# Where a hybrid decoder step casts and splits its weights around a norm: last lower parts behind the last residual sum, the memory's parts behind the inverse root

## The chip, the cores and the metric

The kernel runs on one core of a Trainium2 chip. The time is the device time of one launch in microseconds (us); the kernel before was timed in three runs, and one more execution was recorded by the hardware profiler. TensorE (PE) multiplies, VectorE (DVE), ScalarE (ACT) and GpSimd (POOL) do the elementwise work, SyncE (SP) issues the loads.

## The reference

One step of a decoder trunk of two layers over a prompt of 256 rows and 8 single sample rows, which share the weights (so 264 columns go through each projection). All of it is float32.

```python
def rmsnorm(x, g):
    y = x * lax.rsqrt(jnp.mean(x * x, axis=-1, keepdims=True) + EPS)
    return y * g

def cross_attn(x, mk, mv, w_q, w_o):
    q = (x @ w_q).reshape(B, T, X_HEADS, X_HEAD_DIM)          # 4 heads of 256
    s = jnp.einsum('bthd,bnhd->bhtn', q, mk) / math.sqrt(X_HEAD_DIM)
    p = jax.nn.softmax(s, axis=-1)
    o = jnp.einsum('bhtn,bnhd->bthd', p, mv).reshape(B, T, D)
    return o @ w_o
...
# layer i, D = 1024, D_FF = 2816:
x += 0.5 * swiglu(rmsnorm(x, norm_ffn1[i]), ...)
x += short_conv_mixer(...) if i is even else hgrn2_mixer(...)   # of rmsnorm(x, norm_mix[i])
x += cross_attn(rmsnorm(x, norm_xattn[i]), mk, mv, ...)
x += 0.5 * swiglu(rmsnorm(x, norm_ffn2[i]), ...)
# the prompt's mk, mv = split(rmsnorm(mem_prompt, norm_mem[i]) @ w_kv[i]); the samples' come from a cache
```

## The kernel before

The activations stand transposed, as xT of 8 tiles of 128 features by 264 columns. PE multiplies in float32r, a rounded float32, and each float32 product is made of three: high times high, low times high and high times low (mm3, lines 330 to 332: `wh`·`xh`, `wh`·`xl`, `wl`·`xh`). So every operand is kept as a rounded part (named with h) and the remainder (with l).

The weights come in parts of 512 KB by SP (raw). ACT casts each to its rounded part (wh, line 107), and DVE, or in some stages GpSimd, subtracts to get the lower part (wl, line 120). The class Weights does this ahead of use: the program is written as one sequence of products, and after every few of them `flow.tick()` is called, which first lets the weights `advance()` by one split, one cast and some loads, and then takes one step of each of three lists of generators (lanes). The emission order and a scheduler that keeps data dependences set the order on each engine. `W.behind(engine, instruction)` adds an order on one engine, without a wait: the instruction stands behind the one noted in `W.after[engine]`.

A norm is spread over the work around it. When a residual tile xT[k] is summed (by `evac` in `out_proj`, line 825, or in `ffn`, line 817), `nxt.kt(k)` makes its high part (ACT, line 350), its low part (DVE, line 355) and its square (ACT, line 366; POOL adds the squares into nacc, line 367). After the last tile the generator `finish` is started on lane 2: three ticks later ACT rounds the sum (nhi, line 376) and DVE makes its remainder (nlo, line 377), one tick later PE sums over the features (ps_ms, lines 380 and 381), ACT takes the logarithm and the exponential for the inverse root (line 310), where the next stage needs another function set loads it (a table load, line 306: silu for the ffn norms, sigmoid for the mixer norm of layer 1; the other three norms here load none), and DVE does a Newton step in three instructions (lines 321, 325, 326) that give R. The projections do not wait for R: their columns are scaled by R when a bank of PSUM is evacuated (g in `ffn`, qT at line 927). `project` starts the first two chunks of 256 output features interleaved, which takes all four banks named "mm"; the third chunk needs an evacuated bank. `out_proj` of attention goes through `project_late`, which multiplies the first three heads of the input before the last.

In `attention`, `mem_split` (lines 909 to 922) makes high and low parts of the memory on ACT (mh, line 918) and DVE (ml, line 919), `do_kv` makes keys and values of the prompt's memory from them for each head (kv, lines 941 to 943), and `sample_scores` reduces the cached keys on DVE (line 995, 128 reductions). `sample_rest` goes on with pst (lines 1069 to 1080), spv (line 1097, products with the cached values in groups of 32), copies to os (line 1108), transposes spt (line 1112), and oh and ol (lines 1115, 1116), which the output projection needs. pkt, psc, ppt and po belong to the prompt's heads.

Of the kernel before, what the change touches and what calls it, by code (L numbers as in the profile page):

```python
# [11 lines left out]
AF = mybir.ActivationFunctionType  # L12
ALU = mybir.AluOpType
# [5 lines left out]
KT = D // P  # L19
# [18 lines left out]
W_BUFS = 5  # L38
# [18 lines left out]
class Weights:  # L57


    def __init__(self, nc, pool):  # L60
        self.nc, self.pool = nc, pool
        self.halves, self.chunks = [], []
        self.raw, self.ready = {}, {}
        self.n_load = self.n_round = self.n_split = self.first_live = self.pos = 0
        self.lo, self.hi = ("v",), ("s",)
        self.pin = lambda ins: ins
        self.order, self.after = None, {}

    def add(self, *srcs):

# [63 lines left out]

    def advance(self):
        n = len(self.halves)
        if self.n_split < self.n_round:
            self._split()
        if self.n_round < n and self.n_round - self.first_live < W_BUFS:
            self._round()  # L140
        while self.n_load < n and self.n_load - self.n_split < RAW_BUFS:
            self._load()
# [97 lines left out]
def trunk_step(ctx: ExitStack, tc: tile.TileContext, ins, consts, outs, stop=None):  # L240
    nc = tc.nc
# [11 lines left out]
    def aux_bank(name):  # L253
        return paux.tile([P, 512], F32, tag="aux", name=name)

    W = Weights(nc, wp)
# [22 lines left out]
    memT = cp.tile([P, KT, NMEM], F32, name="memT")  # L279
    xh = cp.tile([P, KT, NC], F32R, name="xh")  # L280
    xl = cp.tile([P, KT, NC], F32R, name="xl")

    def gcol(name, layer, kt):
        r = ROW0[name] + layer
        return gains[:, kt, r : r + 1]
# [18 lines left out]
    def use_set(name):  # L304
        if loaded[0] != name:
            in_line(nc.scalar.preload_act_table_set(name))
            loaded[0] = name
# [4 lines left out]
    def rsqrt(dst, src, scale=1.0):  # L312

        n = dst.shape[0]
        use_set(LNEXP)
        act(dst, src, AF.Ln, bias=eps_t[:n], scale=scale)
        act(dst, dst, AF.Exp, scale=-0.5)

    def newton(dst, src, tmp, scale=1.0, out=None):
        if scale == 1.0:  # L320
            nc.vector.scalar_tensor_tensor(tmp, src, EPS, dst, op0=ALU.add, op1=ALU.mult)
        else:
            nc.vector.tensor_scalar(tmp, src, scale, EPS, op0=ALU.mult, op1=ALU.add)
            nc.vector.tensor_mul(tmp, tmp, dst)
        nc.vector.scalar_tensor_tensor(tmp, tmp, -0.5, dst, op0=ALU.mult, op1=ALU.mult)
        return nc.vector.scalar_tensor_tensor(dst if out is None else out, tmp, 1.5, dst, op0=ALU.add, op1=ALU.mult)
# [7 lines left out]
    class Norm:  # L334
# [17 lines left out]
        def low(self, k, src=None, n=NC):  # L352
            src = xT[:, k] if src is None else src
            g, h = gcol(self.name, self.layer, k), xh[:, k, :n].bitcast(F32)
            W.pin(nc.vector.scalar_tensor_tensor(xl[:, k, :n], src, g, h, op0=ALU.mult, op1=ALU.subtract))  # L355

        def split(self, k, src, n):
            self.high(k, src, n)
# [12 lines left out]
        def finish(self):  # L371
            yield
            yield
            yield
            hi, lo = (cp.tile([P, NC], F32R, tag="nsq", name=n, bufs=2) for n in ("nhi", "nlo"))
            nc.scalar.copy(hi, self.acc)
            nc.vector.tensor_sub(lo, self.acc, hi.bitcast(F32))
            yield
            ps = aux_bank("ps_ms")
            nc.tensor.matmul(ps[:, :NC], ones_d, hi, start=True, stop=False)  # L380
            nc.tensor.matmul(ps[:, :NC], ones_d, lo, start=False, stop=True)
            with tc.high_priority(offset=HURRY):
                rsqrt(self.R, ps[:, :NC])
                W.after["s"] = last[0]
                if self.after is not None:
                    use_set(self.after)
                W.after["v"] = newton(self.R, ps[:, :NC], self.acc).ins
            self.done = True
# [64 lines left out]
    def project_late(nch, rh, rl, evac, k0, ready):  # L453

        lead = 3
        first = W.chunks[W.pos]
        ws = [W.get_late() for _ in range(lead)]
        pss = [[(mm_bank if c < 2 else aux_bank)(f"pj{c}_{j}") for j in range(2)] for c in range(lead)]

        def block(c, k):  # L460
            for j in range(2):
                mm3(pss[c][j][:, :NC], ws[c](k), rh[:, k], rl[:, k], k == 0, k == KT - 1, slice(j * P, j * P + P))

        for k in range(k0):
            for c in range(2):
                block(c, k)
            if k == HK - 1:
                W.first_live = first[0] + 2
            flow.tick()
        for k in range(k0):  # L470
            block(2, k)
            if k == HK - 1:
                W.first_live = first[1]
            if k % 2:
                flow.tick()
        ready()

        def leave(c, j, ps):
            with tc.high_priority(offset=HURRY):
                evac(c, j, ps[:, :NC])  # L480

        def finish(c):
            for k in range(k0, KT):
                block(c, k)
            W.first_live = first[1] + c + 1
            for j in range(2):
                leave(c, j, pss[c][j])
            flow.tick()

        for c in range(lead - 1):  # L490
            finish(c)
        w = W.get_late()
        for j in range(2):
            ps = mm_bank(f"pj{lead}_{j}")
            for k in range(KT):
                mm3(ps[:, :NC], w(k), rh[:, k], rl[:, k], k == 0, k == KT - 1, slice(j * P, j * P + P))
                if k == KT // 2 - 1:
                    flow.tick()
            if j == 1:
                W.release()  # L500
            leave(lead, j, ps)
            flow.tick()
            if j == 0:
                finish(lead - 1)
# [315 lines left out]
            flow.drain(1)  # L820

    def out_proj(rh, rl, nxt, before=None, late=None):
        def evac(c, j, ps):
            k = 2 * c + j
            add = nc.vector.tensor_add(xT[:, k], xT[:, k], ps)
            if k == KT - 1:
                W.after["v"] = add.ins
                nxt.low(k - 1)
            nxt.kt(k, low=k != KT - 2)

        if late is not None:
            project_late(4, rh, rl, evac, *late)
        else:
            project(4, rh, rl, evac, before=before)


    def conv(norm, nxt):
        with tc.tile_pool(name="cv", bufs=1) as vp:
# [54 lines left out]

            flow.spawn(0, states())
            out_proj(yh, yl, nxt)
            flow.drain(0)


    def attention(l, norm, nxt):
        with tc.tile_pool(name="at", bufs=1) as ap:  # L900
            mh = ap.tile([P, KT, NMEM], F32R, name="mh")
# [11 lines left out]
            def mem_split():  # L913
                for _ in range(6):
                    yield
                for k in range(KT):
                    g = gcol("norm_mem", l, k)
                    nc.scalar.activation(mh[:, k], memT[:, k], AF.Copy, scale=g)
                    nc.vector.scalar_tensor_tensor(
                        ml[:, k], memT[:, k], g, mh[:, k].bitcast(F32), op0=ALU.mult, op1=ALU.subtract  # L920
                    )
                    yield

            def evac_q(h, j, ps):
# [137 lines left out]
            def sample_rest():  # L1062
# [53 lines left out]
                nc.vector.tensor_sub(olv, ptv, ohv.bitcast(F32))  # L1116

            flow.spawn(1, mem_split())
            project(XH, xh, xl, evac_q, need=norm)
            W.lo = ("p",)  # L1120
            for h in range(XH):
                do_kv(h)
            flow.drain(0)
            W.lo = ("v",)
            out_proj(oh, ol, nxt, late=(KT - 2, lambda: flow.drain(1)))


    GH = 4

    def rec(norm, nxt):  # L1130
        with tc.tile_pool(name="rc", bufs=1) as rp:
# [303 lines left out]
            def before(k):  # L1435
                while k not in made:
                    flow.step()

            out_proj(lambda k: yh[k // GH][:, k % GH], lambda k: yl[k // GH][:, k % GH], nxt, before=before)

    def states():
# [109 lines left out]
    for i, e in enumerate(plan):  # L1551
        if i + 1 < len(plan):
            nxt = Norm(*plan[i + 1][:3])
        else:
            nxt = Final() if stop is None else Stop()
# [60 lines left out]
```

## Time and profile before

| | before |
|---|---|
| time, median of 3 runs | 1294.13 us (1294.10 to 1295.05) |
| profiled execution: time | 1294.04 us |
| its span | 1292.3 us |
| granted TensorE clock | 0.998 |
| PE busy | 1270.8 us, 98% of the span |
| DVE, ACT, POOL busy | 824.0, 691.8, 293.3 us |
| bytes moved | 270.98 MB, mean 210 GB/s |

The span is the time from the first to the last instruction on the core. A row of the timeline has the start, the duration, the engine, the line and operation, the tile written and those read, and in brackets how long the engine was idle before it and what ended that. Rows of several like instructions carry their count (x3). In a list of waits the columns are the time in total, how often, and the longest. Matmul rows overlap (0.28 us long, started every 0.12).

### The profile page before, as it was taken

The page shows a single profiled execution, that of the slowest core. Times are in us where ns is not written, and L with a number is a line of the kernel's source. Part 1 is how long each engine was busy: PE and PEld are TensorE (multiplying, and loading weights), DVE is VectorE, ACT ScalarE, POOL GpSimd, SP SyncE. Part 2 cuts the span into 40 slices and gives each one's busy share as a digit, 9 for nine tenths or more (in the row PEclk, how much of TensorE's full clock was granted, in tenths as well). Part 3 has the DMA queues.
Part 4 walks back from the last instruction along what each step waited for, and adds up shares of the span by engine and source line. Part 5 has one row for each costly group of instructions (what it writes and reads, how often), then busy time and mean ns, then how long its engine had stood idle before and what let it go on. Part 6 is the DMA issues. An engine that isn't in the chain of part 4 may idle for free.

```text
span 1292.3 us, 25853 instructions
## 1 busy us (share of the span) xinstructions
PE 1270.8 (98%) x10267; PEld 1232.6 (95%) x10267; DVE 824.0 (64%) x1560; ACT 691.8 (54%) x1131; POOL 293.3 (23%) x237
## 2 busy tenths in 40 slices
PE   8999999999999999999999999999999999999996
PEld 8999999999869999999999999999998789999996
DVE  7555567759926755546655545887888628766454
ACT  6454545446545655544645544656575546766542
POOL 3211231212650211132111132000023531112220
PEclk9999999999999999999999999999999999999999
DMA  8796555646998666556666556563547995997551
GB/s 279 236 304 180 166 181 181 198 147 196 358 369 254 187 175 189 174 163 196 188 181 179 185 167 194 172 194 108 189 151 242 392 359 149 291 314 240 163 164 35
DMA packets 263755, 270.98 MB, mean 210 GB/s; under 512 B 8777, under 2 KB 259721, under 8 KB 261074
## 3 DMA queue, kind: packets, MB, share of 16 engines
q1 hardware_dynamic: 257726, 263.98, 64.4%
q10 hardware_dynamic: 5908, 5.35, 1.2%
q8 instruction: 81, 1.33, 0.4%
q14 instruction: 40, 0.33, 0.1%
HBM read 259.19 MB, written 10.10 MB: 208 GB/s over the span
## 4 chain that ended last, share of the span: by engine, by line
PE 92%; DVE 4%; ACT 2%; issue 1%; DMA 0%; POOL 0%; DVEq 0%; SPq 0%; ACTq 0%; POOLq 0%
PE pj L330 19%; PE pj L331 19%; PE pj L332 19%; PE dn L330 7%; PE dn L332 7%; PE dn L331 7%; PE kv L942 2%; PE kv L941 2%; PE kv L943 2%; DVE xl L355 2%; DVE wl L120 1%; PE spv L1097 1%; PE psc L1023 1%; PE pl L1263 1%; PE pj L408 1%
## 5 line engine op out<-in xcount | busy, mean ns | idle before, releaser
L120 DVE TENSOR_TENSOR wl<-raw,wh 128x1024 fp32r<-128x1024 f32 (+1 forms) x347 | 424.6, 1229 | 242.8 <-ACT wh L107 230.0
L330 PE MATMUL pj<-xh,wh 128*128 128x264 f32 x1952 | 558.4, 286 | 5.0 <-DVE qT L927 2.6
L331 PE MATMUL pj<-xl,wh 128*128 128x264 f32 x1952 | 553.3, 284 | 0.0
L332 PE MATMUL pj<-xh,wl 128*128 128x264 f32 x1952 | 553.1, 283 | 0.0
L107 ACT CAST wh<-raw 128x1024 fp32r<-128x1024 f32 (+1 forms) x406 | 415.9, 1032 | 251.2 <-PE pj L331 123.1
L330 PEld LDWEIGHTS pj<-xh,wh 128*128 128x128 f32 x1952 | 367.7, 188 | 7.3 <-DVE qT L927 3.0
L331 PEld LDWEIGHTS pj<-xl,wh 128*128 128x128 f32 x1952 | 367.9, 189 | 0.0
L332 PEld LDWEIGHTS pj<-xh,wl 128*128 128x128 f32 x1952 | 366.2, 188 | 0.0
L330 PE MATMUL dn<-ah,wh 128*128 128x264 f32 x704 | 200.9, 285 | 0.0
L332 PE MATMUL dn<-ah,wl 128*128 128x264 f32 x704 | 200.0, 284 | 0.0
L331 PE MATMUL dn<-al,wh 128*128 128x264 f32 x704 | 199.5, 283 | 0.0
L120 POOL TENSOR_TENSOR wl<-raw,wh 128x1024 fp32r<-128x1024 f32 (+1 forms) x61 | 142.9, 2351 | 183.9 <-ACT wh L107 120.0
L791 POOL TENSOR_TENSOR al<-a,ah 128x264 fp32r<-128x264 f32 x88 | 89.2, 1015 | 412.6 <-ACT ah L790 412.4
L332 PEld LDWEIGHTS dn<-ah,wl 128*128 128x128 f32 x704 | 132.7, 188 | 0.0
L330 PEld LDWEIGHTS dn<-ah,wh 128*128 128x128 f32 x704 | 132.4, 188 | 0.2
L331 PEld LDWEIGHTS dn<-al,wh 128*128 128x128 f32 x704 | 132.5, 188 | 0.0
L310 ACT ACTIVATE g<-g 128x264 f32<-128x264 f32 x88 | 37.0, 424 | 76.2 <-DVE g L783 76.0
L790 ACT CAST ah<-a 128x264 fp32r<-128x264 f32 x88 | 36.0, 413 | 70.4 <-DVE a L789 70.1
L350 ACT ACTIVATE xh<-xT,gains 128x264 fp32r<-128x264 f32 x56 | 28.2, 513 | 74.2 <-DVE xT L817 59.2
L995 DVE CUSTOM_DVE_ANT_0 junk<-ring,pq 128x256 f32<-128x256 f32 x128 | 53.6, 419 | 3.7
L783 DVE TENSOR_TENSOR g<-pj,R_norm_ffn 128x264 f32<-128x264 f32 x88 | 37.4, 429 | 28.7 <-PE pj L332 28.3
L789 DVE TENSOR_TENSOR a<-g,pj 128x264 f32<-128x264 f32 x88 | 37.0, 424 | 26.7 <-PE pj L332 26.7
(325 smaller groups left out, 1477.4 us busy)
## 6 DMA issues: line engine op xcount, KB each, us to landing
raw<-in_w_ffn_gate_dram SPq DMA_DIRECT2D x88, 512.0 KB, 6.0
raw<-in_w_ffn_up_dram SPq DMA_DIRECT2D x88, 512.0 KB, 3.9
raw<-in_w_ffn_down_dram SPq DMA_DIRECT2D x64, 512.0 KB, 3.5
ring<-in_cache_mem_k_dram SPq DMA_DIRECT2D x16, 1024.0 KB, 8.7
raw<-in_w_xkv_dram SPq DMA_DIRECT2D x64, 256.0 KB, 3.9
ring<-in_cache_mem_v_dram SPq DMA_DIRECT2D x16, 1024.0 KB, 8.5
raw<-in_w_rec_in_dram SPq DMA_DIRECT2D x32, 512.0 KB, 4.4
raw<-in_w_ffn_down_dram SPq DMA_DIRECT2D x32, 384.0 KB, 3.0
```

The source lines that it names most:

```text
L107: self.pin(self.behind(self.hi[i % len(self.hi)], copy(wh[:, :n], self.raw[i][:, :n])))
L120: ins = eng.tensor_sub(wl[:, :n], self.raw.pop(i)[:, :n], wh[:, :n].bitcast(F32))
L310: in_line(nc.scalar.activation(dst, src, func, **kw))
L330: nc.tensor.matmul(ps, wh[:, s], rh, start=first, stop=False)
L331: nc.tensor.matmul(ps, wh[:, s], rl, start=False, stop=False)
L332: nc.tensor.matmul(ps, wl[:, s], rh, start=False, stop=last)
L350: W.pin(nc.scalar.activation(xh[:, k, :n], src, AF.Copy, scale=gcol(self.name, self.layer, k)))
L783: nc.vector.tensor_mul(g, ps, norm.R)
L789: nc.vector.tensor_mul(a, g, ps)
L790: nc.scalar.copy(ah[:, blk], a)
L791: nc.gpsimd.tensor_sub(al[:, blk], a, ah[:, blk].bitcast(F32))
L995: nc.vector.tensor_tensor_reduce(junk, t[:, i % 8], pq[:, :XD], 1.0, 0.0, ALU.mult, ALU.add, sc[:, h, i : i + 1])
```

## The change

Three edits. `W.held` is set between the step of `finish` that makes nhi and nlo and the step with ps_ms, and no weight part is cast or split in between. In `out_proj`, the low parts of the last tiles (6 and 7; in attention's projection 4 to 7) stand behind the last residual sum. The memory's high parts stand behind the norm's exponential and its low parts behind the Newton step.

```diff
     def advance(self):
         n = len(self.halves)
-        if self.n_split < self.n_round:
+        if not self.held and self.n_split < self.n_round:
             self._split()
-        if self.n_round < n and self.n_round - self.first_live < W_BUFS:
+        if not self.held and self.n_round < n and self.n_round - self.first_live < W_BUFS:
             self._round()
...
             nc.vector.tensor_sub(lo, self.acc, hi.bitcast(F32))
+            W.held = True
             yield
+            W.held = False
             ps = aux_bank("ps_ms")
...
     def out_proj(rh, rl, nxt, before=None, late=None):
+        later = range(KT - 2 if late is None else KT - 4, KT - 1)
+
         def evac(c, j, ps):
             k = 2 * c + j
             add = nc.vector.tensor_add(xT[:, k], xT[:, k], ps)
+            nxt.kt(k, low=k < later[0])
             if k == KT - 1:
                 W.after["v"] = add.ins
-                nxt.low(k - 1)
-            nxt.kt(k, low=k != KT - 2)
+                for i in (*later, k):
+                    W.behind("v", nxt.low(i))
...
-                    nc.scalar.activation(mh[:, k], memT[:, k], AF.Copy, scale=g)
-                    nc.vector.scalar_tensor_tensor(
+                    W.behind("s", nc.scalar.activation(mh[:, k], memT[:, k], AF.Copy, scale=g))
+                    low = nc.vector.scalar_tensor_tensor(
                         ml[:, k], memT[:, k], g, mh[:, k].bitcast(F32), op0=ALU.mult, op1=ALU.subtract
                     )
+                    W.behind("v", low)
                     yield
```

What that moves in the order of the engines is shown at three places of layer 0. A name carries the number of its buffer, which differs between the two programs where it is a written one; a raw with the same number is the same weight part. Line numbers of after are one to seven higher (mh stands at line 924 there, spv at 1104, spt at 1119).

ACT at the norm before attention, before:

```order
L918 ACTIVATE mh<-memT,gains 128x256 x2
L376 CAST nhi<-nacc_norm_xattn_2599 128x264
L918 ACTIVATE mh<-memT,gains 128x256 x6
L107 CAST wh_3896<-raw_3680 128x1024
L310 ACTIVATE R_norm_xattn_2600<-ps_ms,eps_t 128x264
L310 ACTIVATE R_norm_xattn_2600<-R_norm_xattn_2600 128x264
L107 CAST wh_3920<-raw_3702 128x1024
L107 CAST wh_3974<-raw_3754 128x1024
```

and after:

```order
L377 CAST nhi<-nacc_norm_xattn_2599 128x264
L310 ACTIVATE R_norm_xattn_2600<-ps_ms,eps_t 128x264
L310 ACTIVATE R_norm_xattn_2600<-R_norm_xattn_2600 128x264
L107 CAST wh_3916<-raw_3680 128x1024
L107 CAST wh_3932<-raw_3702 128x1024
L924 ACTIVATE mh<-memT,gains 128x256 x6
L107 CAST wh_3974<-raw_3754 128x1024
L993 COPY zq<-qT_3968 128x256
```

All eight mh casts and one weight cast (raw_3680) stood ahead of the logarithm and the exponential (the two rows of line 310); now only nhi stands there, and six of the mh stand behind two weight casts.

PE at the end of attention (kv: keys and values; pj: the output projection's first chunks), before:

```order
L941 MATMUL kv_0_4761<-wh_4694,mh 128x512
L1112 MATMUL spt<-ident,os 128x128 x2
L971 MATMUL pkt<-ident,Kn_4724 128x128 x4
L942 MATMUL kv_0_4761<-wl_4736,mh 128x512
L943 MATMUL kv_0_4761<-wh_4694,ml 128x512
L941 MATMUL kv_1_4762<-wh_4694,mh 128x512
L942 MATMUL kv_1_4762<-wl_4736,mh 128x512
L1023 MATMUL psc<-KTt_4783,qT_4017 128x256 x4
L943 MATMUL kv_1_4762<-wh_4694,ml 128x512
L330 MATMUL pj_0_4898<-oh,wh_4738 128x264
```

and after:

```order
L948 MATMUL kv_1_4762<-wh_4694,mh 128x512
L949 MATMUL kv_1_4762<-wl_4736,mh 128x512
L950 MATMUL kv_1_4762<-wh_4694,ml 128x512
L1104 MATMUL spv<-ring_4645,Ps 8x256 x4
L1104 MATMUL spv<-ring_4643,Ps 8x256 x8
L1104 MATMUL spv<-ring_4645,Ps 8x256 x4
L1119 MATMUL spt<-ident,os 128x128 x2
L978 MATMUL pkt<-ident,Kn_4724 128x128 x4
L330 MATMUL pj_0_4898<-oh,wh_4738 128x264
```

Six kv products stood between the last spv and spt (the last of them is the first row here), and five behind pkt; now the last spv group stands behind all of them, and the projection follows pkt directly.

From the output projection of attention to the norm of the second ffn, DVE, before:

```order
L825 TENSOR_TENSOR xT<-xT,pj_1_4903 128x264
L120 TENSOR_TENSOR wl_5207<-raw_4918,wh_5192 128x1024
L355 SCALAR_TENSOR_TENSOR xl<-xT,gains,xh 128x264 x3
L825 TENSOR_TENSOR xT<-xT,pj_1_5194 128x264
L120 TENSOR_TENSOR wl_5240<-raw_4996,wh_5230 128x1024
L355 SCALAR_TENSOR_TENSOR xl<-xT,gains,xh 128x264
L120 TENSOR_TENSOR wl_5274<-raw_5012,wh_5258 128x1024
L377 TENSOR_TENSOR nlo<-nacc_norm_ffn_3813,nhi 128x264
```

and after:

```order
L830 TENSOR_TENSOR xT<-xT,pj_1_4903 128x264
L120 TENSOR_TENSOR wl_5205<-raw_4918,wh_5190 128x1024
L830 TENSOR_TENSOR xT<-xT,pj_1_5192 128x264
L355 SCALAR_TENSOR_TENSOR xl<-xT,gains,xh 128x264 x4
L120 TENSOR_TENSOR wl_5240<-raw_4996,wh_5230 128x1024
L120 TENSOR_TENSOR wl_5274<-raw_5012,wh_5258 128x1024
L378 TENSOR_TENSOR nlo<-nacc_norm_ffn_3813,nhi 128x264
```

The last residual sum (the row on pj_1_5194, after pj_1_5192) moved ahead of the low parts xl; between it and nlo stand the same instructions as before in another order.

ACT at the same norm, before:

```order
L376 CAST nhi<-nacc_norm_ffn_3813 128x264
L107 CAST wh_5306<-raw_5078 128x1024
L310 ACTIVATE R_norm_ffn_3814<-ps_ms,eps_t 128x264
L310 ACTIVATE R_norm_ffn_3814<-R_norm_ffn_3814 128x264
L306 ACT_TABLE_LOAD
L107 CAST wh_5331<-raw_5132 128x1024
L107 CAST wh_5389<-raw_5149 128x1024
```

and after:

```order
L377 CAST nhi<-nacc_norm_ffn_3813 128x264
L310 ACTIVATE R_norm_ffn_3814<-ps_ms,eps_t 128x264
L310 ACTIVATE R_norm_ffn_3814<-R_norm_ffn_3814 128x264
L306 ACT_TABLE_LOAD
L107 CAST wh_5327<-raw_5078 128x1024
L107 CAST wh_5343<-raw_5132 128x1024
L107 CAST wh_5389<-raw_5149 128x1024
```

The cast of raw_5078 moved from ahead of the logarithm to behind the table load. The orders of SP and POOL do not change, apart from the line numbers.

More of the change, by code (lines that the diff above doesn't have):

```diff
@@ L66, in __init__ @@
         self.pin = lambda ins: ins
-        self.order, self.after = None, {}
+        self.order, self.after, self.held = None, {}, False
     def add(self, *srcs):
@@ L354, in low @@
             g, h = gcol(self.name, self.layer, k), xh[:, k, :n].bitcast(F32)
-            W.pin(nc.vector.scalar_tensor_tensor(xl[:, k, :n], src, g, h, op0=ALU.mult, op1=ALU.subtract))
+            ins = nc.vector.scalar_tensor_tensor(xl[:, k, :n], src, g, h, op0=ALU.mult, op1=ALU.subtract)
+            return W.pin(ins) or ins
         def split(self, k, src, n):
```

## The prediction

> **What bounds the kernel.** I read the page first, then the list of waits, then the timelines of TensorE (PE), ScalarE (ACT) and VectorE (DVE) around each norm and at the end of attention. Line numbers here are those of the kernel before.
>
> ```profile
> PE 1270.8 (98%) x10267; PEld 1232.6 (95%) x10267; DVE 824.0 (64%) x1560; ACT 691.8 (54%) x1131; POOL 293.3 (23%) x237
> ```
>
> PE is busy for 1270.8 of 1292.3 us, and so the whole span is a row of products with a few gaps. An edit that moves work on ACT and DVE can only gain what PE waits for today, and can lose by making new gaps. The waits of PE that this change touches are few (us in total, how often, longest):
>
> ```profile
> PE pj L330 <- DVE qT L927: 2.6, 2, 1.5
> PE pj L330 <- DVE xT L825: 2.4, 2, 1.2
> ...
> PE pst L1073 <- DVE tops L1071: 0.3, 2, 0.2
> ```
>
> 2.6 + 2.4 + 0.3 = 5.3 us is the most that the listed waits can give back, 0.4% of the time; each gap also costs about 0.1 us of slower first product (a matmul row of 0.39 instead of 0.28). I go through the places in turn, as differences in PE's time.
>
> **1. Norm before attention: the wait for qT goes.** Products start every 0.12 us; after the gap the third chunk's first product starts:
>
> ```profile
> 313.53 0.29 PE L331 MATMUL pj<-xl,wh 128*128 128x264 f32 x1
> 313.66 0.28 PE L332 MATMUL pj<-xh,wl 128*128 128x264 f32 x1
> 314.95 0.39 PE L330 MATMUL pj<-xh,wh 128*128 128x264 f32 x1 [1.02 <-DVE qT L927]
> ```
> ```profile
> 976.74 0.28 PE L332 MATMUL pj<-xh,wl 128*128 128x264 f32 x1
> 978.56 0.39 PE L330 MATMUL pj<-xh,wh 128*128 128x264 f32 x1 [1.54 <-DVE qT L927]
> ```
>
> Without a gap they would have started at 313.78 and 976.86, so the gaps are 1.17 and 1.70 us. What came late is on ACT: the mean square was ready early, but six casts of the memory and a weight cast stood ahead of the logarithm.
>
> ```profile
> 307.73 0.40 PE L381 MATMUL ps_ms<-nlo,ones_d 128*128 128x264 f32 x1
> ```
> ```profile
> 306.60 2.51 ACT L918 ACTIVATE mh<-memT,gains 128x256 fp32r<-128x256 f32 x6
> 309.02 1.04 ACT L107 CAST wh<-raw 128x1024 fp32r<-128x1024 f32 x1
> 309.96 0.47 ACT L310 ACTIVATE R_norm_xattn<-ps_ms,eps_t 128x264 f32<-128x264 f32 x1
> ```
>
> ps_ms ended at 308.13 and the logarithm began at 309.96, 1.8 us later. Behind it DVE does three Newton steps, two weight splits and then the evacuation:
>
> ```profile
> 307.60 3.24 DVE L919 SCALAR_TENSOR_TENSOR ml<-memT,gains,mh 128x256 fp32r<-128x256 f32 x8
> ...
> 312.20 2.35 DVE L120 TENSOR_TENSOR wl<-raw,wh 128x1024 fp32r<-128x1024 f32 x2
> 314.48 1.44 DVE L927 TENSOR_TENSOR qT<-pj,R_norm_xattn 128x264 f32<-128x264 f32 x4
> ```
>
> With memory and weight casts behind the exponential, the logarithm begins at about 308.17, DVE is through its Newton steps by 312.20 - 1.79 = 310.41, two splits take 314.48 - 312.20 = 2.28, and one ml (3.24 / 8 = 0.40, pipelined 0.35) now stands ahead of the first qT: 310.41 + 2.28 + 0.35 = 313.04. PE needed 314.95 - 314.48 = 0.47 from there, so it could go at 313.51, ahead of the 313.78 at which it arrives. The gap closes in layer 0. In layer 1 the same casts leave the ACT queue and the gap is longer; I take it all too. Gain 1.17 + 1.70, and 0.1 each for the slow first product: **-3.0 us** (from -1.5, if the new ml work keeps half of it, to -3.1).
>
> The moved ml's do not vanish: eight of them, 3.24 us, ran on DVE where it waited for ACT anyway, and now stand among the evacuations and score reductions behind R. I cost that at nothing, since DVE's rows there come ahead of what PE wants; what it costs if that cover fails is a rival.
>
> **2. Output projection of attention: the bank wait moves, it does not go.**
>
> ```profile
> 423.90 0.28 PE L332 MATMUL pj<-xh,wl 128*128 128x264 f32 x1
> 425.39 0.39 PE L330 MATMUL pj<-xh,wh 128*128 128x264 f32 x1 [1.21 <-DVE xT L825]
> ```
> ```profile
> 428.92 0.39 PE L381 MATMUL ps_ms<-nlo,ones_d 128*128 128x264 f32 x1
> ```
>
> PE's first ffn product waits 1.4 us (425.39 against 424.02) for the last residual sum to free its bank; the list of waits counts two such waits, 2.4 us, and the second is layer 1's. DVE had three lower parts in front of it:
>
> ```profile
> 421.08 1.21 DVE L120 TENSOR_TENSOR wl<-raw,wh 128x1024 fp32r<-128x1024 f32 x1
> 422.22 2.77 DVE L355 SCALAR_TENSOR_TENSOR xl<-xT,gains,xh 128x264 fp32r<-128x264 f32 x3
> 424.92 0.41 DVE L825 TENSOR_TENSOR xT<-xT,pj 128x264 f32<-128x264 f32 x1
> ...
> 428.45 0.42 DVE L377 TENSOR_TENSOR nlo<-nacc_norm_ffn,nhi 128x264 fp32r<-128x264 f32 x1
> ```
>
> The sum now goes ahead of the lower parts, to about 422.3, and the bank is free before PE asks for it. But DVE has no idle time from 421.08 to the cast remainder nlo at 428.45, and what stands between is the same set of instructions in another order: one split, four lower parts, one sum, two splits. So nlo still comes at 428.45 + 0.42 = 428.87, and the ps_ms product that needs it stands at the same row of PE. It started at 428.92, only just in time; 1.4 us earlier PE will stand and wait for it. The wait goes from xT to nlo. I take -0.2 for each layer, for lower parts that meet less GpSimd work: **-0.4 us** (bounds: -1.4 each, if nlo comes as much earlier; +0.3 each, if the lower parts get slower).
>
> ACT's cast between nhi and the logarithm leaves too, but the logarithm there waited for ps_ms and not for the cast, so this alone gives nothing.
>
> **3. End of attention: the last sample products lose their cover.** The order of PE shows that the last group of spv, and the transposes spt and pkt, now stand behind the last kv product and straight before the output projection's first product. Before:
>
> ```profile
> 384.43 1.91 PE L1097 MATMUL spv<-ring,Ps 128*8 128x256 f32 x32
> 386.27 0.50 PE L942 MATMUL kv<-wl,mh 128*128 128x512 f32 x1
> ...
> 387.95 0.44 PE L1112 MATMUL spt<-ident,os 128*128 128x128 f32 x2
> 388.23 0.60 PE L971 MATMUL pkt<-ident,Kn 128*128 128x128 f32 x4
> 388.58 0.48 PE L942 MATMUL kv<-wl,mh 128*128 128x512 f32 x1
> ```
> ```profile
> 386.41 1.49 ACT L1108 COPY os<-spv 8x256 f32<-8x256 f32 x4 [1.01 <-PE spv L1097]
> 388.43 0.21 ACT L1115 CAST oh<-spt 128x64 fp32r<-128x64 f32 x1 [0.53 <-PE spt L1112]
> ```
> ```profile
> 388.67 0.23 DVE L1116 TENSOR_TENSOR ol<-spt,oh 128x64 fp32r<-128x64 f32 x1 [11.58 <-ACT oh L1115]
> ```
>
> ACT copies os out of the bank from 386.41, which takes until 387.90, and spt starts at 387.95. In that time PE did six kv products, from 386.27. These stand ahead of spv now, and nothing is left between spv and spt: PE idles 387.95 - 386.27 = 1.68. Then the first projection product needs oh, and the second ol, which ended at 388.90, that is 0.95 after spt began; spt and pkt cover 388.58 - 387.95 = 0.63, and one product 0.12, which leaves about 0.2. Less about 0.2 for two restarts of kv products that no longer come behind spv and pkt (first rows of 0.50 and 0.48), some 1.65 for each layer: **+3.3 us** (bounds: 1.4 and 2.0 each). The pkt that stands beside it covers a wait of its own, not this one.
>
> Earlier, spv's first half is cut into more pieces between kv products, and pst and its scores stand some 13 products later. Each break costs a restart (the row of 0.50 above). **+0.4 us**, bounds 0 and +1, the upper end by the tops wait (0.2 at its longest) coming back at each of four steps.
>
> **4. A weight cast behind the table load.** Where a norm is followed by a table load, the cast that stood ahead of the logarithm now stands behind the load. At the second ffn of layer 0:
>
> ```profile
> 429.35 0.48 ACT L310 ACTIVATE R_norm_ffn<-ps_ms,eps_t 128x264 f32<-128x264 f32 x1 [0.19 <-PE ps_ms L381]
> ...
> 430.31 1.28 ACT L306 ACT_TABLE_LOAD   x1
> 431.60 1.05 ACT L107 CAST wh<-raw 128x1024 fp32r<-128x1024 f32 x1
> ```
> ```profile
> 431.61 2.35 DVE L120 TENSOR_TENSOR wl<-raw,wh 128x1024 fp32r<-128x1024 f32 x2
> 434.06 0.80 DVE L783 TENSOR_TENSOR g<-pj,R_norm_ffn 128x264 f32<-128x264 f32 x2
> ```
> ```profile
> 434.60 0.28 PE L330 MATMUL pj<-xh,wh 128*128 128x264 f32 x1
> ```
>
> DVE's two splits began at 431.61, straight behind the last Newton step, on casts that were done. Now the first of them needs the cast that begins at 431.60: 431.60 + 1.05 + 0.04 = 432.69, and g starts 2.28 later (as in part 1), at 434.97, and PE 0.47 behind it, at 435.44. It arrived at 434.60: a new gap of 0.84, and 0.1 for the slow first product. The first ffn of layer 1 has the same rows:
>
> ```profile
> 623.72 1.06 ACT L107 CAST wh<-raw 128x1024 fp32r<-128x1024 f32 x1
> ```
> ```profile
> 626.18 0.80 DVE L783 TENSOR_TENSOR g<-pj,R_norm_ffn 128x264 f32<-128x264 f32 x2
> ```
> ```profile
> 626.72 0.28 PE L330 MATMUL pj<-xh,wh 128*128 128x264 f32 x1
> ```
>
> 623.72 + 1.06 + 0.04 + 2.28 + 0.47 = 627.57 against 626.72, 0.85. The recurrent mixer has a load too and I price it alike. At the last ffn only one split stands ahead of g in the new order, and the norms of the conv mixer and of attention load no table: nothing. **+2.7 us** (bounds 0, if the order of DVE lets g pass, and 3.5 with the last ffn).
>
> [...]
>
> SP's and GpSimd's own orders do not change. The ring loads behind the last spv come as late as spv, about 2.5 us; the weight parts queued behind them on SP are wanted by ACT only when PE frees a buffer, which I cost at nothing (at most 0.5 in each layer).
>
> **Sum.** -3.0 - 0.4 + 3.3 + 0.4 + 2.7 = **+3.0 us**, against the profiled execution's 1294.04, which is 0.09 under the median of the runs: **1297.0 us**. A change under 0.2%, 2.6 us, is about what a measurement of this kernel cannot tell from none.
>
> **Rivals.**
> - Part 2's gain is real (0.11). If nhi and nlo come earlier because GpSimd's sums end sooner, the two bank waits are won whole: -2.8 in place of -0.4, +0.6, 1294.6. Against it stands DVE without idle time up to nlo.
> - The other side: part 3 costs nothing (0.08). If the ACT copies of os ran beside spv's last products, or PE had seven products to run, there is no stall, +3.0 - 3.0 = 0.0, 1294.0, not slower. It decides once 1.68 us of other work stands between spv and spt; the rows show that the copies begin at 386.41, when spv's last row has ended (384.43 + 1.91 = 386.34), and the order shows no other work.
> - Part 4's cast does not hold g (0.05): +0.3, 1294.3. For it speaks that today g ends only just in time (434.06 + 0.47 = 434.53 for a product at 434.60), so that PE and not the splits may set it; against it that two splits stand ahead of g.
> - DVE backlog (0.08). Eight ml's among the score reductions, 3.24 us, push mxs and pst back; if half of it reaches PE in each layer, +3.2 more, 1300.2.
> - ACT is held behind each table load for as long as the load itself took, 1.28 (0.02): three norms, +3.8, 1300.8. The row of the cast, 1.29 behind the load's start, speaks against it. [...]
> - The first three rivals together, or two of them with the low ends of their bounds (0.04): 3.0 - 2.4 - 3.0 - 2.7 = -5.1, 1288.9, to -2.6.
> The remaining 0.62 is the forecast, with its own range +1.6 to +4.6, 1295.6 to 1298.6; 0.45 of it lies over +2.6.
>
> Slower: 0.45 + 0.08 + 0.02 = 0.55. Within 0.2%: 0.17 + 0.11 + 0.08 + 0.05 = 0.41. Faster: 0.04. The range takes in the rivals near no change and most of the backlog: 1293.5 to 1299.8.
>
> **What would show it.** Right: no wait for qT at the third chunk; the wait for xT gone and one of about 1.3 us for nlo at ps_ms, in both layers; spt waiting about 1.6 us for os twice; a wait of about 0.8 us for g twice and for G once. Wrong: nlo starting before 428 by more than half a microsecond, a wait for tops or for kv's parts above 1 us, or a g that starts where it did.

## The result, and the profile after

The changed kernel takes 1301.09 us (median of 6 runs, 1300.69 to 1304.18) against 1294.7 us before (6 runs), so by the medians it is 6.4 us slower; the ratio of the means is 1.0054, 95% interval 1.0044 to 1.0064. Forecast were 3.0 us more, 1297.0, with a range of 1293.5 to 1299.8; the time lies above it. The profiled execution of the changed kernel was the longest of the six, 1304.18 us; a second profile of the same kernel took 1300.56 us, and both are used below. The kernel before was timed again beside each group of experiments (medians 1294.25 to 1294.67 us), and each ratio is against those runs. Line numbers in rows of after are those of the changed kernel.

```profile
span 1302.3 us, 25835 instructions
...
PE 1278.2 (98%) x10267; PEld 1236.4 (95%) x10267; DVE 821.6 (63%) x1560; ACT 691.8 (53%) x1131; POOL 295.4 (23%) x237
```

PE's waits in this execution, by what ended them (us in total, how often, longest):

```profile
PE spt L1119 <- ACT os L1115: 3.2, 2, 1.6
...
PE ps_ms L384 <- DVE nlo L378: 2.2, 2, 1.1
PE ppt L1044 <- DVE Pp L1022: 1.7, 4, 0.7
...
PE pj L330 <- DVE g L786: 0.6, 2, 0.3
...
PE pj L330 <- DVE G L1171: 0.3, 1, 0.3
```

The waits for qT and xT (5.0 us before) are gone from the list. In their place stand 3.2 for os, 2.2 for nlo, 1.7 for Pp, and 0.9 for g and G. All but Pp had been forecast, those for os and nlo within 0.2 for each, those for g and G at more than twice their size. The end of attention in layer 0, on PE and on ACT:

```profile
392.02 0.44 PE L1119 MATMUL spt<-ident,os 128*128 128x128 f32 x2 [1.61 <-ACT os L1115]
392.29 0.60 PE L978 MATMUL pkt<-ident,Kn 128*128 128x128 f32 x4
```
```profile
390.48 1.49 ACT L1115 COPY os<-spv 8x256 f32<-8x256 f32 x4 [0.78 <-PE spv L1104]
392.49 0.21 ACT L1122 CAST oh<-spt 128x64 fp32r<-128x64 f32 x1 [0.53 <-PE spt L1119]
```

The copies take their 1.49 us as before, but PE has nothing else to do until 392.02.

What the list of waits doesn't show is the clock. In windows of 1 us (length, PE busy and its instructions, granted clock, DMA share, GB/s) behind this wait:

```profile
393.00:394.00 1.00, 1.00 (x6) 0.68 1.22 291
394.00:395.00 1.00, 1.00 (x6) 0.50 1.21 291
395.00:396.00 1.00, 1.00 (x4) 0.50 1.27 301
396.00:397.00 1.00, 1.00 (x4) 0.62 1.14 283
397.00:398.00 1.00, 1.00 (x9) 1.00 1.15 321
```

PE is busy in each of these rows, at half its clock from about 393.4 to 396.8. In layer 1 the same happens behind the same wait. In the second profile of the same kernel it happens in neither layer, though the wait is as long:

```profile
PE spt L1119 <- ACT os L1115: 3.2, 2, 1.6
...
PE ppt L1044 <- DVE Pp L1022: 1.4, 2, 0.7
```
```profile
393.00:397.00 4.00, 4.00 (x28) 1.00 1.21 291
```

So the profile first read here holds two stretches of 3.4 us at half clock, about 1.7 us of lost time each, that not every execution has; 1304.18 less 1300.56 is 3.6.

To place the loss I took the starts of the same PE rows in each profile, less those of before (us). The columns are the changed kernel's second profile and its three edits alone, which the next section describes; pq is the first use of qT, dn the first down projection product of an ffn, pl a product of the recurrent mixer behind its norm, the last row the end of PE's work.

| PE row | before | changed | memory alone | held alone | low parts alone |
|---|---|---|---|---|---|
| ps_ms, norm before attention 0 | 307.53 | +0.04 | -0.02 | +0.11 | +0.27 |
| pq, attention 0 | 316.54 | -0.99 | -1.34 | -0.04 | +1.04 |
| ps_ms, second ffn of layer 0 | 428.75 | +1.60 | +2.82 | +0.09 | -0.37 |
| dn, second ffn of layer 0 | 550.97 | +3.41 | +2.80 | +0.66 | +0.86 |
| dn, first ffn of layer 1 | 743.09 | +4.00 | +2.80 | +1.26 | +0.86 |
| pl, mixer 1 | 830.80 | +4.60 | +2.80 | +1.86 | +0.86 |
| ps_ms, norm before attention 1 | 970.48 | +4.45 | +2.82 | +1.73 | +0.91 |
| pq, attention 1 | 980.14 | +2.71 | +1.04 | +1.09 | +0.94 |
| ps_ms, second ffn of layer 1 | 1092.41 | +5.33 | +5.15 | +1.29 | -0.59 |
| end | 1282.70 | +6.82 | +5.19 | +1.55 | +0.67 |

With the memory's edit alone, each attention from pq to the next ps_ms loses 4.2 us (2.82 + 1.34) and 4.1 (5.15 - 1.04). That is the whole loss; the norms in front of them win 1.3 and 1.8.

### The profile page after: what moved, and what is told of

It reads as the page before. It is cut to its first block, busy times and chain, and to the rows that moved or that the text cites. A ratio compares the mean times of both kernels' runs of the same rounds, so it can differ in the third digit from the quotient of the medians.

```text
span 1302.3 us, 25835 instructions
## 1 busy us (share of the span) xinstructions
PE 1278.2 (98%) x10267; PEld 1236.4 (95%) x10267; DVE 821.6 (63%) x1560; ACT 691.8 (53%) x1131; POOL 295.4 (23%) x237
## 4 chain that ended last, share of the span: by engine, by line
PE 89%; DVE 6%; ACT 2%; DMA 1%; issue 1%; POOL 0%; DVEq 0%; SPq 0%; ACTq 0%; POOLq 0%
PE pj L330 19%; PE pj L331 18%; PE pj L332 18%; PE dn L330 7%; PE dn L332 7%; PE dn L331 7%; DVE wl L120 2%; PE kv L950 2%; PE kv L949 2%; PE kv L948 2%; DVE xl L355 2%; PE spv L1104 1%; PE psc L1030 1%; PE pl L1270 1%; ACT wh L107 1%
## 5 line engine op out<-in xcount | busy, mean ns | idle before, releaser
L368 POOL TENSOR_TENSOR nacc_norm_xattn<-nacc_norm_xattn,nsq 128x264 f32<-128x264 f32 x14 | 14.6, 1044 | 174.7 <-ACT nsq L367 174.3
```

## The experiments

Theory A: the loss comes from the order of PE's products in attention, which the memory's edit alone makes. Theory B: it comes from the weight casts behind the table loads. First the three edits one by one. The memory's edit:

```diff
-                    nc.scalar.activation(mh[:, k], memT[:, k], AF.Copy, scale=g)
-                    nc.vector.scalar_tensor_tensor(
+                    W.behind("s", nc.scalar.activation(mh[:, k], memT[:, k], AF.Copy, scale=g))
+                    low = nc.vector.scalar_tensor_tensor(
...
+                    W.behind("v", low)
```

> The kernel before with one of the three edits: the memory's high parts behind the exponential, its low parts behind the Newton step. Theory A (the loss comes from the order of products that this edit makes in attention): the wait for qT goes, -2.5; the stall of spt on os comes, +3.3, with the waits of ppt for Pp, +1.6, and some more restarts, +1.5; where the granted clock drops behind the stall, up to +3.3 more. In all +3.9 to +7, 1298 to 1302 us. Theory B (the loss comes from the casts behind the table loads, and this edit gains its qT waits): -2.5, 1292 us.

Measured: 1299.49 us against 1294.51, 1.0040 (1.0027 to 1.0052), +5.0. Theory B falls: this edit, which moves no weight cast behind a table load, holds most of the loss. The wait for os is 3.2, that for Pp 1.4, and no low clock stands behind it (the mean over the span is 0.997, before 0.998, and 0.994 in the profile with two such stretches). What the expectation called restarts is one group of spv in three pieces, on PE:

```profile
364.54 0.64 PE L1098 MATMUL spv<-ring,Ps 128*8 128x256 f32 x4
365.11 0.50 PE L944 MATMUL kv<-wh,ml 128*128 128x512 f32 x1
365.54 0.60 PE L1098 MATMUL spv<-ring,Ps 128*8 128x256 f32 x2
366.07 0.49 PE L942 MATMUL kv<-wh,mh 128*128 128x512 f32 x1
366.50 1.89 PE L1098 MATMUL spv<-ring,Ps 128*8 128x256 f32 x26
```

A whole group of 32 takes 1.84 us (384.43 to 386.27 before). Here 364.54 to 368.32, where the next product starts, is 3.78; less two kv products of 0.23 that is 3.3, so the two cuts cost 1.5; in layer 1 the group is cut in the same way. And the wait for Pp, by DVE and GpSimd, first before and then with this edit:

```profile
348.20 0.61 DVE L1015 TENSOR_SCALAR Pp<-Pp,zsp 128x256 f32<-128x256 f32 x2
```
```profile
348.69 4.77 POOL L120 TENSOR_TENSOR wl<-raw,wh 128x1024 fp32r<-128x1024 f32 x2 [2.16 <-ACT wh L107]
```
```profile
347.56 1.27 DVE L1016 TENSOR_SCALAR Pp<-Pp,zsp 128x256 f32<-128x256 f32 x1
```
```profile
346.28 2.40 POOL L120 TENSOR_TENSOR wl<-raw,wh 128x1024 fp32r<-128x1024 f32 x1 [1.06 <-ACT wh L107]
```

Before, both halves of Pp took 0.61 together, and GpSimd's next weight split began at 348.69, as they ended. With the edit ACT makes the weight cast ahead of the softmax's exponentials instead of behind them; the second exponential and the cast before, then the cast and the first exponential with the edit:

```profile
347.12 0.47 ACT L310 ACTIVATE Pp<-psc,mxp 128x256 f32<-128x256 f32 x1
...
347.57 1.05 ACT L107 CAST wh<-raw 128x1024 fp32r<-128x1024 f32 x1
```
```profile
345.15 1.05 ACT L107 CAST wh<-raw 128x1024 fp32r<-128x1024 f32 x1 [3.66 <-PE kv L944]
346.11 0.47 ACT L310 ACTIVATE Pp<-psc,mxp 128x256 f32<-128x256 f32 x1
```

So the split begins at 346.28, and the first half of Pp, started at 347.56, ends at 348.83, 0.15 after the split does (348.68): 1.27 for one half. PE waits 0.7 for it. Before, the same meeting stood at the second head: there the first half took 1.47 us from 364.76, beside a split from 363.69 to 366.08, and PE did not wait for it. No run moved the split alone. 1.6 for os, 0.7 for Pp and 1.5 for the cuts are 3.8 of the 4.2 us in layer 0.

The second edit alone (nothing cast or split between nhi and ps_ms):

```diff
             nc.vector.tensor_sub(lo, self.acc, hi.bitcast(F32))
+            W.held = True
             yield
+            W.held = False
```

> The kernel before with the second edit alone: no weight part is cast or split between nhi and ps_ms. Theory A: a new wait for g or G of 0.5 with its restart at three norms, +1.7, and at the norm before attention the weight cast leaves the place ahead of the logarithm, about 0.9 less of the qT wait in each layer, -1.9: in all -0.2, 1294.3 us, no clock drop. Theory B: +5 to +6, about 1300 us.

Measured: 1295.40 us, 1.0006 (0.9997 to 1.0015), which can't be told from no change. The profile has both parts: +0.6 at each of three norms with a table load (rows dn, dn and pl above) and 0.26 at the last, against only -0.15 and -0.65 at the norms before attention. There the expectation was wrong, since it saw only ACT's queue. DVE's row:

```profile
307.73 3.25 DVE L921 SCALAR_TENSOR_TENSOR ml<-memT,gains,mh 128x256 fp32r<-128x256 f32 x8
310.90 0.42 DVE L321 SCALAR_TENSOR_TENSOR nacc_norm_xattn<-ps_ms,R_norm_xattn 128x264 f32<-128x264 f32 x1
```

The exponential's result was there at 310.05 (it began at 309.63 and took 0.42), but the eight ml's still stand ahead of the Newton step until 310.9. Both the mh's on ACT and the ml's on DVE have to go for the qT wait to go.

The third edit alone:

```diff
...
+            nxt.kt(k, low=k < later[0])
             if k == KT - 1:
                 W.after["v"] = add.ins
-                nxt.low(k - 1)
-            nxt.kt(k, low=k != KT - 2)
+                for i in (*later, k):
+                    W.behind("v", nxt.low(i))
```

> The kernel before with the third edit alone: the last low parts of an output projection behind its last residual sum. Both theories: the two waits for xT go, -2.8, and two waits of about 1.1 for nlo at ps_ms come, +2.4 with their restarts: -0.4, 1294.1 us. If nlo came earlier by as much, -2.8, 1291.7 us.

Measured: 1294.46 us, 0.9999 (0.9990 to 1.0008): no change. The waits are as expected, with xT gone and nlo in its place:

```profile
PE ps_ms L382 <- DVE nlo L378: 2.3, 2, 1.1
...
PE pj L330 <- DVE qT L931: 3.0, 2, 1.5
```

The table shows -1.41 and then +1.23 in layer 0 (from pq to ps_ms, and from there to dn), -1.53 and +1.26 in layer 1 (to the end); the rest of the difference is a longer qT wait in layer 0, told in the last section. The three edits alone sum to 5.0 + 0.9 - 0.05 = 5.8 of the 6.4 us.

A version that keeps what costs nothing: weight parts are held only where no table load follows, the memory's parts stay where they were.

```diff
-            W.held = True
+            W.held = self.after is None
```

> The low parts of the last tiles behind the last residual sum, and weight parts held back only at norms that no table load follows; the memory's parts as in the kernel before. Theory A: the qT waits lose 0.9 each, no new wait for g, the bank waits move to nlo: -1.9 - 0.4 = -2.3, 1292.2 us. Theory B says the same here within 0.5, so that a time above 1294 would speak against both.

Measured: 1293.23 us, 0.9990 (0.9981 to 0.9998): 1.3 faster, a gain of half the size expected, for the reason just shown (with the second edit the qT waits lost 0.65 and 0.15, not 0.9 each). Against the second edit alone it is 2.2 us less, mostly from the norms with table loads, since the low parts' edit, which it has too, changed nothing alone.

Then the wait for os and the clock. From here on theory A also says that the low clock follows from PE standing idle between spv and spt, and theory C that it has nothing to do with that place. The changed kernel again:

> The changed kernel again, unaltered, as the one to compare with. Theory A (the clock drop follows from PE standing idle between spv and spt): in the profiled execution the granted clock falls to about a half for some 3 us behind spt in at least one layer, or stays at 1.00; times spread from 1300.7 to 1304, with the low clock in the longer ones. Theory C (the clock drop has nothing to do with that place): if it drops at all, it does so elsewhere.

Measured: 1301.49 us (1300.56 to 1302.38), 1.0056 (1.0041 to 1.0070). Its profile, the shortest of its runs, has no low clock (its mean over the span is 0.998) and is still 6.5 us above the profile of before, so the loss does not need it.

The changed kernel with 14 products in the gap (FILL) whose result nobody reads:

```diff
+                for n in range(FILL):
+                    pad = nc.tensor.matmul(pt[:, 2 * P :], ones_d, mh[:, n % KT], start=True, stop=True)
+                    order(pad, tail.ins, "pad")
+                    tail = pad
...
+                    order(t, tail.ins, "pad")
```

> The changed kernel with 14 more products of 128 by 256 in each layer, which nobody reads, between the last spv and spt, so that PE works while os is copied. Theory A: spt stands at the same time or 0.2 later, the wait for os falls from 1.6 to under 0.3, and the granted clock stays at 1.00 there in every execution; the time is at the low end of the changed kernel, 1300.5 to 1301, and its spread under 1 us. Theory C: the clock drops as often as before, spread about 3 us.

Measured: 1300.99 us (1300.71 to 1302.12), 1.0052 (1.0037 to 1.0066). The wait for os is gone from the list and the clock is 1.00 at both places, as theory A has it (the mean over the span is 0.997, with 0.50 from 12 to 15 us, at the kernel's start); but so it is in the kernel without the fill in its second profile, and the spread was 1.4 and not under 1. For the cause of the low clock this settles nothing.

Two of the four copies of os on DVE:

```diff
-                    nc.scalar.copy(os[32 * h : 32 * h + NB], ps[32 * h : 32 * h + NB, :XD])
+                    copy = nc.vector.tensor_copy if h % 2 else nc.scalar.copy
+                    copy(os[32 * h : 32 * h + NB], ps[32 * h : 32 * h + NB, :XD])
```

> The changed kernel with two of the four copies of os on DVE, so that the copies take about half as long. Theory A: the wait of spt falls from 1.6 to about 0.8 in each layer, -1.6, and the clock stays at 1.00: 1298.8 to 1299.3. If the wait is not the copies' (DVE comes late to them), the time stays at 1300.7 and the row names DVE. Theory C: -1.6 on the median, and the spread stays.

Measured: 1303.44 us, 1.0073 (1.0059 to 1.0086), slower, against every theory. The copies did not run side by side. DVE:

```profile
390.89 0.42 DVE L1116 COPY os<-spv 8x256 f32<-8x256 f32 x1
391.74 0.43 DVE L1116 COPY os<-spv 8x256 f32<-8x256 f32 x1 [0.43 <-ACT os L1116]
```

Each of its two copies waited for one on ACT and the other way round, so the wait of spt grew from 1.6 to 1.9. The clock dropped behind it in layer 1 only, to 0.74 and 0.69 in the windows of 3 us from 1060 to 1066; the mean over the span is 0.996.

Every copy of os made twice:

> The changed kernel with each copy of os made twice, so that the copies take about twice as long. Theory A: the wait of spt grows to about 3.1 in each layer, +3.0, and the granted clock drops behind it in both layers in every execution, +1.6 each: 1306.5 to 1307.5. Theory C: +3.0 alone, about 1304.

Measured: 1306.9 us (1305.37 to 1308.78), 1.0097 (1.0083 to 1.0111). The wait is 3.2 in each layer, and the clock drops behind both; in layer 0, in windows as above:

```profile
394.00:397.00 3.00, 2.49 (x12) 0.50 1.21 290
397.00:400.00 3.00, 3.00 (x10) 0.50 1.21 292
```

In layer 0 the low clock lasts 6.8 us (393.56 to 400.39), in layer 1 3.4 (1065.98 to 1069.40), as behind the wait of 1.6. The median is theory A's time (theory C said 1304). That the clock drops in both layers in every execution, as theory A had it, is not shown: only one of the four has a profile, and it is the longest.

Next, the memory's edit with the cover put back: the last 18 kv products stand behind the last spv group.

```diff
+                        if h == XH - 1 and k >= KT - 3:
+                            W.behind("p", mm)
...
+                    W.after["p"] = mm.ins
```

> The kernel with the memory's edit alone, and beside it 18 kv products of the last head put behind the last spv group, so that six of them stand between it and spt again, as in the kernel before. Theory A (of that edit's +5.0 some 3.4 is the lost cover): the wait of spt for os goes in both layers, 1296.1 us, with the first spv group still in three pieces and the wait of ppt for Pp still 0.7. Theory D (the loss is the moved DVE work as such, and PE's wait only shows it): the wait appears at another place, and the time stays within 1 of 1299.5.

Measured: 1297.36 us (1295.42 to 1298.39), 1.0015 (1.0006 to 1.0024); its profiled execution took 1296.36. The wait for os is gone, and no other grew by as much:

```profile
PE pj L330 <- DVE xT L825: 2.4, 2, 1.2
PE ppt L1040 <- DVE Pp L1018: 1.9, 3, 0.7
```

By the medians, each against its own runs of before, the loss falls from 5.0 to 2.7 us, so 2.3 come back; by the profiles' ends 3.0 (5.19 to 2.22), of 3.4 expected. Theory D, by which the time stays within 1 of 1299.5, falls: the lost cover is a cost of its own. In attention 2.9 and 2.2 us are left (4.2 and 4.1 with the memory's edit alone). That is the cuts (1.5) and the wait for Pp (0.7) in each layer, and in layer 0 another wait for Pp of 0.45.

Last, the version that keeps what costs nothing, from above, with nhi and nlo put ahead of the second of the two weight splits:

```diff
-            nc.scalar.copy(hi, self.acc)
-            nc.vector.tensor_sub(lo, self.acc, hi.bitcast(F32))
+            with tc.high_priority(offset=HURRY):
+                nc.scalar.copy(hi, self.acc)
+                nc.vector.tensor_sub(lo, self.acc, hi.bitcast(F32))
```

> The low parts behind the last residual sum, weight parts held back only where no table load follows, and nhi and nlo given a higher priority, which puts nlo ahead of the last of the two weight splits at the norms of the second ffn and changes nothing at the other norms' DVE. If DVE's queue sets nlo, as the prediction's second part has it: the waits of ps_ms for nlo fall from 1.1 to under 0.3 in both layers, -2.0 against the version without it, 1291.2 us. If nlo then waits for nhi, -1.0. If the split that now stands behind nlo makes PE wait, no gain.

Measured: 1290.78 us (7 runs, 1290.54 to 1291.69), 0.9970 (0.9959 to 0.9981): 3.9 us faster than before, and the fastest of all. Against the version without that priority it is about 2.5 us less, where 2.0 were expected. The wait for nlo has left the list; DVE's order is now:

```profile
425.69 1.78 DVE L120 TENSOR_TENSOR wl<-raw,wh 128x1024 fp32r<-128x1024 f32 x1
427.39 0.42 DVE L379 TENSOR_TENSOR nlo<-nacc_norm_ffn,nhi 128x264 fp32r<-128x264 f32 x1
427.73 1.21 DVE L120 TENSOR_TENSOR wl<-raw,wh 128x1024 fp32r<-128x1024 f32 x1
```

So DVE's queue did set nlo, and with nlo one split earlier the low parts' edit gives what its diff seemed to offer.

## Why the prediction was wrong

The direction was right, the size was not: +3.0 forecast, +6.4 measured. By its steps, against the second profile's +6.8 (clock at 1.00):

- Part 1, the qT waits: -3.0 forecast, -1.03 and -1.74 measured, -2.8. The size was right. The reading that ACT was what came late is half of it: with ACT freed by the second edit alone, DVE's eight ml's still held the Newton step until 310.9. The change moves both. The memory's edit alone gave -1.32 and -1.78.
- Part 2, the bank wait moves to nlo: -0.4 forecast, -0.18 and -0.27 measured with the edit alone. Right, and the experiment on nlo shows the mechanism.
- Part 3, the lost cover: 1.65 forecast for each layer; the wait for os was 1.6, and putting the cover back returned 2.3 to 3.0 of 3.3. Right.
- The second paragraph of part 3 is the step that failed: "spv's first half is cut into more pieces" and pst and scores stand later, +0.4 with bounds 0 and +1. In attention the memory's edit cost 4.2 and 4.1 us; less part 3's 1.65 each that is 5.0 in all where +0.4 stood. The cuts of one spv group cost 1.5 in each layer (a restart was priced at 0.1), and the wait for Pp, which the prediction doesn't have, 0.7. The order of ACT shows the weight cast that moved ahead of the exponentials there; I had read only PE's order at that place. These two make 4.4 of the 5.0; the other 0.6 are not placed, and no run undid the cuts or the early cast alone: their sizes are read from the rows.
- Part 4, a cast behind the table load: +2.7 forecast, +0.6 at three norms and 0.26 at the last, +2.0 measured. The chain on ACT and DVE came as forecast; what was wrong is the time at which PE arrives:

```profile
435.03 1.28 ACT L306 ACT_TABLE_LOAD   x1
436.33 2.00 ACT L107 CAST wh<-raw 128x1024 fp32r<-128x1024 f32 x2
```
```profile
437.41 2.36 DVE L120 TENSOR_TENSOR wl<-raw,wh 128x1024 fp32r<-128x1024 f32 x2 [0.99 <-ACT wh L107]
439.69 0.77 DVE L786 TENSOR_TENSOR g<-pj,R_norm_ffn 128x264 f32<-128x264 f32 x2
```
```profile
439.56 0.28 PE L332 MATMUL pj<-xh,wl 128*128 128x264 f32 x1
440.17 0.39 PE L330 MATMUL pj<-xh,wh 128*128 128x264 f32 x1 [0.33 <-DVE g L786]
```

From the table load (435.03) to the split 2.38 and to g 4.66; forecast 432.69 - 430.31 = 2.38 and 434.97 - 430.31 = 4.66. The term was too large because the row of 434.60 was not the third chunk's first product: the order has 48 products between ps_ms and it, and I had counted 45 rows. It starts three products later:

```profile
434.96 0.29 PE L330 MATMUL pj<-xh,wh 128*128 128x264 f32 x1
```

By that row the gap is 435.44 - 434.96 = 0.48; measured 440.17 - 439.68 = 0.49.

So 2.8 + 0.5 of gains and 3.3 + 2.0 of losses came about as said within 1 us in all, and the 5.0 that the failed step held made the result. Two of the rivals came near the time, by other mechanisms: ACT held behind each table load (0.02, 1300.8 us), which the row of the cast refutes (it began at 436.33, 1.30 us after the load at 435.03, and the load itself took 1.28), and the backlog on DVE (0.08, 1300.2 us). With the memory's edit alone PE waited only 0.2 us for tops; the loss came not from the volume of the moved ml's but from the order of PE and ACT that this edit brought.

## What to carry to other kernels

Where an order-only dependency moves work on two engines, read the whole stretch of every engine until the orders agree again, not only the places that the edit names: here about half of what was lost stood some 35 to 55 us behind the norm, in a group of small products cut in three and in a weight split on GpSimd that now ran at the same time as a piece of softmax on DVE. With the low parts' edit alone the wait that was taken away from one buffer (xT, 2.4 us before) came back at the next thing in the same queue (nlo, 2.3 us); look for that one, and move it too, before judging an edit. Count rows from the program's order when a start time carries a term.

## What the runs showed of the hardware

- Half clock behind a short gap. Behind PE's wait for os the granted clock fell to 0.50 at five of the ten places that have this wait: at two of six with 1.6 us (both layers of one profile, none in two others), one of two with 1.9, two of two with 3.2. In the seven profiles without this wait the mean granted clock of the span was 0.997 or 0.998, against 0.994 in the profile above; in the kernel before it was 1.00 at both places. With the fill, and with the doubled copies, it also fell from 12 to 15 us, at the kernel's start (0.50 and 0.55). In the profile above it lasted from about 393.36 (0.68 in the first window) to 396.76 (0.62 in the last), 3.4 us.
- The length of the wait alone does not decide. In the 3.41 us ahead of both drops of the profile above (389.94 to 393.35 and 1058.95 to 1062.37) PE idled 1.61 us; in the second profile it waited the same 1.6 us for os in both layers and the clock held; with two copies on DVE the clock held in layer 0 behind a wait of 1.9. The low stretches of the profile above begin 669.02 us apart (393.35 and 1062.37), those with the doubled copies 672.42 (393.56 and 1065.98): the two distances differ by 3.40, about the length of one stretch. What sets where a stretch begins is not shown. Nor is it shown that the wait is the cause, by a run that takes it away: the one that filled the gap had no low clock at these places, but neither had the second profile, without the fill.
- Two cuts in a group of 8-column products by 128-column products cost 1.5 us here, 0.7 each, against the 0.1 us of a restart in the prediction. What of it is the switch and what the breaking of the group is not shown.
- GpSimd and DVE starting an operation together: on GpSimd the last sum of squares before attention, before and after:

```profile
305.33 0.92 POOL L367 TENSOR_TENSOR nacc_norm_xattn<-nacc_norm_xattn,nsq 128x264 f32<-128x264 f32 x1 [1.47 <-ACT nsq L366]
```
```profile
305.48 1.81 POOL L368 TENSOR_TENSOR nacc_norm_xattn<-nacc_norm_xattn,nsq 128x264 f32<-128x264 f32 x1 [1.47 <-ACT nsq L367]
```
```profile
305.46 1.22 DVE L120 TENSOR_TENSOR wl<-raw,wh 128x1024 fp32r<-128x1024 f32 x1
```

Before, GpSimd began at 305.33, ahead of a weight split of DVE at 305.56 that took 1.77; after, the split began at 305.46, 0.02 ahead, and took 1.22, and GpSimd's sum 1.81. Most sums of that line on GpSimd took 0.75 or 0.76, and the splits on DVE just before these 1.21. So in both cases the one that started first took near its usual time (0.92 and 1.22), and the other 0.56 and 1.05 longer than usual. Such a race of 0.1 us moved nhi by 1.0 us (307.33 against 306.29); in the low parts' edit alone the same sum took 1.82 and the qT wait was the longer. The first half of Pp is a second case: in the profiles of before, of the memory's edit alone and with the cover, and the two of the changed kernel, the ten halves that took 1.25 to 1.47 us, and not about 0.35, each ended 0.14 to 0.16 after a GpSimd split that had started before them.
